# A two-block network on one core: the first mixer's head norms, its attention one step later, and its weights split ahead

## The chip, the core and the metric

The program runs on one core of one Trainium2 chip. The metric is the device time of one execution in microseconds. TensorE (PE) multiplies, VectorE (DVE) and ScalarE (ACT) work element by element, SyncE (SP) issues every DMA. Each engine runs its own list of instructions in order and waits on semaphores for the others.

## The reference, cut to what matters

Two blocks over 512 tokens of width 1024, all float32: a gated feed-forward layer (f1), a first mixer (m1), a second feed-forward layer (f2), then four more stages. The change touches f1 and m1. With the constants put in, m1 is:

```python
h = rmsnorm(x, norm_mix)
xr, gr, q, k, v, ga, gb = split(h @ w_in)            # seven parts of 1024 columns
xc = dwconv(xr)                                      # 4 taps
y_lru = (lru_scan(xc) + lru_scan_backward(xc)) * gelu(gr)   # gates of 64x64 blocks, sqrt, scan
q = rmsnorm(q per head of 64) * q_norm * 64**-0.5    # 16 heads
k = rmsnorm(k per head of 64) * k_norm
y_att = softmax(q k^T + bias over a window of 8 x 16) v
x = x + (sigmoid(ga) * y_lru + sigmoid(gb) * y_att) @ w_out
```

## The kernel before

Activations lie with the features on the 128 partitions and the 512 tokens along the free axis, so one row of weights `w_in[i]` (128 x 1024, eight blocks of 128 x 128) gives 128 features of one part. To keep float32 accuracy, both operands are split into a high part `hi` in float32r and a rest `lo`; `mm3` (L172 to L177) makes three products per block: hi by hi, lo by hi, hi by lo. A projection (`proj`) is thus 24 products of 512 columns. `wload` (L115) loads 512 KB of weights into `raw`, ACT rounds them to `whi` (L137), DVE subtracts to get `wlo` (L144). `raw`, `whi` and `wlo` have three buffers each.

`presplit` (L149) does the split ahead of time and in DRAM: per block a load into `raw`, two casts on ACT (L160), two subtractions on DVE (L161), and a DMA of the low part to DRAM (L162). From then on `wload` loads `wlo` from there (L142) and DVE has nothing to do. In the kernel before, this is done for two weights of a late stage, 28 blocks, within f2's loop of 22 steps over the hidden width; `raw`'s three buffers are shared between it and the loop's own weights.

m1 works in eight units `unit(m)`, one per pair of heads and 128 channels. A unit projects q, k, xr, v; norms q and k per head; runs the convolution, the four gate products (`lru_gates`, three products each on `xs`) and the scan; then projects gr and ga of unit m-1, gb of unit m-2; and at last scales q and k and stacks them (`stack_q`, `stack_k`). The norm (L760 to L829): the squares of 128 tokens are the stationary operand and a 128 x 2 matrix of ones per head the moving one, so that sums stand as 128 tokens by 16 columns in a bank of the pool `t` (L768); a reciprocal root; a transpose to 16 rows (L804); and eight products of 128 columns with a selecting matrix (L824) spread each root over its 64 partitions.

The attention of unit m, `attention` (L487), is a generator of ten steps. A step makes the logits of one head and 128 queries (kh, kl; L502, L503), their softmax (`softmax`, L577, two buffers of `l`), and the transposes of the step before (L516) with their split into ph and pl (L519, L520); two of the steps make the products with the values (L532). `weave` (L566) takes turns between the pieces of `unit(m)` and the steps of `attend(m - 1)`, so the attention of one unit lies under the projections of the next.

PSUM has eight banks: `m` two (projections, gates), `o` two, `t` four (logits, transposes, spread roots). A scheduler puts each engine's instructions in order from this program order and its own costs; the order is then fixed.

Of the kernel before, what the change touches and what calls it, by code (L numbers as in the profile page):

```python
# [16 lines left out]
P = 128  # L17
S = 512
# [18 lines left out]
class Split:  # L37


    def __init__(self, raw, lo):  # L40
        self.raw, self.lo, self.shape = raw, lo, raw.shape

    def __getitem__(self, i):
        return Split(self.raw[i], self.lo[i])
# [5 lines left out]
class Net:  # L50
# [98 lines left out]
    def presplit(self, name):  # L149
# [3 lines left out]
        self.ins[name] = Split(src, lo)  # L153
        for m in range(src.shape[0]):
# [332 lines left out]
    def attention(self, ap, Q, K, V, blocks, step, logits, out, mask=None, lag=1, bank=None):  # L487
# [7 lines left out]
        for t in range(len(todo) + lag + 1):  # L495
# [25 lines left out]
            if t in (4 + lag, 8 + lag):  # L521
                a = int(t > 4 + lag)
# [54 lines left out]
    def softmax(self, ap, bias):  # L577
        nc = self.nc

        def f(a, b, ps, n):  # L580
            l = ap.tile([P, n], F32, name="l", tag="l", bufs=2)
# [127 lines left out]
    def sigm2(self, ps):  # L709

        s = self.tmp("sg")
        self.nc.scalar.activation(s, ps, AF.Tanh, scale=0.5)
        return s

    def mixer1(self, nxt):
        nc, tc, ins = self.nc, self.tc, self.ins
        w_in = ins["w_in"]
        with ExitStack() as ctx:
# [18 lines left out]
            heads = c1.tile([P, 2], F32, name="heads")  # L737
            nc.sync.dma_start(heads, ins["heads"])
            t = self.wp.tile([P, 1024], F32, name="raw", tag="raw", bufs=3)
            nc.sync.dma_start(t[0:48], ins["sel"])  # L740
            sel = c1.tile([48, 1024], F32R, name="sel")
            nc.scalar.copy(sel, t[0:48])

            sp = c1.tile([48, P], F32R, name="ssp")
            nc.vector.memset(t[0:48, 0:P], 0.0)
            nc.scalar.copy(sp, t[0:48, 0:P])
# [5 lines left out]
            NR = 16  # L752
            roots = c1.tile([P, 2 * S + NR], F32, name="roots")
            ths = [roots[:, d * S : (d + 1) * S] for d in range(2)]
            ss = roots[:, 2 * S :]
            rng = [(0, 2), (0, 3), (1, 4), (2, 4)]
            off = [384, 0, 0, 640]
            HS, YA, QK, VV = {}, {}, {}, {}

            def unit(m):  # L760

                if m < KD:
                    raws, sqs = [], []

                    def sums(w):
                        for b in range(4):
                            o = 8 * w + 2 * b
                            nc.tensor.matmul(  # L768
                                st[:, o : o + 2], sqs[w][:, b * P : (b + 1) * P], heads, start=o == 0, stop=True,
                                skip_group_check=True)  # L770

                    for w in range(2):
# [37 lines left out]
                if 0 <= m - 1 < KD:  # L810
                    self.gelu_times(HS[m - 1], self.proj(w_in[KD + m - 1], h, key="gr"))
                    yield
                    s = self.sigm2(self.proj(w_in[4 * KD + m - 1], h, key="ga"))
# [517 lines left out]
```

## Time and profile before

| | us |
|---|---|
| median of three runs (lowest, highest) | 2467.26 (2466.57, 2468.57) |
| the profiled execution, its own time | 2469.19 |
| its span in the trace | 2467.4 |
| PE busy, of the span | 2403.5 (97%) |
| DVE busy | 1468.1 (60%) |
| ACT busy | 1129.9 (46%) |
| share of PE in the chain that ended last | 84% |

Products on PE are pipelined: a product of 512 columns has a length of 0.39 us in the records but the next begins 0.23 us after it. A busy share near 100% therefore doesn't say that nothing can be won; the starts of the products do. f1 lies from 0 to some 390 us, m1 from there to some 840 us, f2 from 860 to 1230 us. In m1 a unit takes 55.4 us from the third on.

### The profile page before, as it was taken

The numbers are of one execution on the slowest core, as the hardware profiler recorded it, in microseconds if no ns is written. First come the engines' busy times: TensorE is split into PE (matmuls) and PEld (weight loads), VectorE is DVE, ScalarE is ACT, GpSimd is POOL, SyncE is SP. The second block draws the span as 40 slices with busy tenths as digits, with TensorE's granted clock in tenths as the row PEclk, the third lists the DMA queues.
The fourth block names the chain that finished last, engine by engine and source line by source line (L and its number), as shares of the span: only waits on it lengthen the run. The fifth ranks groups of instructions, "written<-read, shape, count | busy, mean of one in ns | idle before, by whom it ended". The sixth has DMA issues, their size and how long they took to land.

```text
span 2467.4 us, 32211 instructions
## 1 busy us (share of the span) xinstructions
PE 2403.5 (97%) x12710; PEld 2048.5 (83%) x12710; DVE 1468.1 (60%) x2524; ACT 1129.9 (46%) x1849; POOL 39.1 (2%) x75
## 2 busy tenths in 40 slices
PE   9999999999999999999999999999999979999998
PEld 8888898777777798888988798888898859888887
DVE  5444347888888755553556665554357996555524
ACT  5223236766666544442355554333246566433322
POOL 0000000000000000000000000000001120000000
PEclk9999999999999999999999999999999999999999
DMA  4232333322222256663432222322344413223233
GB/s 151 94 102 92 94 112 119 95 88 88 80 99 84 86 204 213 214 227 95 117 118 82 85 94 69 102 95 90 101 151 150 145 53 136 69 97 101 90 96 94
DMA packets 83559, 276.08 MB, mean 112 GB/s; under 512 B 9328, under 2 KB 14064, under 8 KB 83408
## 3 DMA queue, kind: packets, MB, share of 16 engines
q1 hardware_dynamic: 83408, 274.03, 34.4%
q8 instruction: 99, 1.62, 0.3%
q14 instruction: 52, 0.43, 0.1%
HBM read 257.20 MB, written 16.80 MB: 111 GB/s over the span
## 4 chain that ended last, share of the span: by engine, by line
PE 84%; DVE 9%; ACT 4%; issue 2%; DMA 1%; POOL 0%; SPq 0%; ACTq 0%; DVEq 0%; POOLq 0%
PE psm L177 15%; PE psm L175 15%; PE psm L176 15%; PE pso L176 10%; PE pso L175 10%; PE pso L177 10%; DVE wlo L144 1%; DVE pso L1063 1%; ACT whi L137 1%; PE pst L516 1%; PE pso L532 1%; PE pst L175 1%; PE pst L176 1%; PE pst L283 1%; PE pst L177 1%
## 5 line engine op out<-in xcount | busy, mean ns | idle before, releaser
L137 ACT CAST whi<-raw 128x1024 fp32r<-128x1024 f32 (+3 forms) x402 | 408.5, 1017 | 770.3 <-issue 340.3
L144 DVE TENSOR_TENSOR wlo<-raw,whi 128x1024 fp32r<-128x1024 f32 (+2 forms) x380 | 447.7, 1179 | 311.0 <-ACT whi L137 309.9
L175 PE MATMUL psm<-hh,whi 128*128 128x512 f32 (+1 forms) x1512 | 573.2, 380 | 4.2 <-ACT hh L326 3.0
L177 PE MATMUL psm<-hl,whi 128*128 128x512 f32 (+1 forms) x1512 | 569.0, 377 | 0.1
L176 PE MATMUL psm<-hh,wlo 128*128 128x512 f32 (+1 forms) x1512 | 569.0, 376 | 0.0
L175 PEld LDWEIGHTS psm<-hh,whi 128*128 128x128 f32 x1512 | 285.7, 189 | 54.1 <-ACT hh L326 3.9
L177 PEld LDWEIGHTS psm<-hl,whi 128*128 128x128 f32 x1512 | 285.7, 189 | 49.7 <-DVE hl L327 0.7
L176 PEld LDWEIGHTS psm<-hh,wlo 128*128 128x128 f32 x1512 | 286.2, 189 | 46.5
L175 PE MATMUL pso<-hh,whi 128*128 128x512 f32 (+1 forms) x728 | 272.8, 375 | 0.9 <-ACT whi L137 0.9
L176 PE MATMUL pso<-hh,wlo 128*128 128x512 f32 (+1 forms) x728 | 272.4, 374 | 0.2 <-DVE wlo L144 0.2
L177 PE MATMUL pso<-hl,whi 128*128 128x512 f32 (+1 forms) x728 | 272.5, 374 | 0.0
L176 PE MATMUL psm<-mh,wlo 128*128 128x512 f32 (+1 forms) x506 | 172.5, 341 | 1.6 <-DVE wlo L144 1.6
L175 PE MATMUL psm<-mh,whi 128*128 128x512 f32 (+1 forms) x506 | 172.1, 340 | 0.0
L177 PE MATMUL psm<-ml,whi 128*128 128x512 f32 (+1 forms) x506 | 172.0, 340 | 0.0
L458 DVE TENSOR_TENSOR md<-pso,gp 128x512 f32<-128x512 f32 x84 | 58.0, 692 | 169.7 <-PE pso L177 168.2
L175 PEld LDWEIGHTS pso<-hh,whi 128*128 128x128 f32 x728 | 137.9, 189 | 25.1 <-ACT whi L137 1.1
L176 PEld LDWEIGHTS pso<-hh,wlo 128*128 128x128 f32 x728 | 137.9, 189 | 24.3 <-DVE wlo L144 0.4
L177 PEld LDWEIGHTS pso<-hl,whi 128*128 128x128 f32 x728 | 137.8, 189 | 24.5 <-issue 0.5
L176 PE MATMUL pso<-mh,wlo 128*128 128x256 f32 (+1 forms) x440 | 145.7, 331 | 1.3 <-DVE wlo L144 1.3
L175 PE MATMUL pso<-mh,whi 128*128 128x256 f32 (+1 forms) x440 | 145.9, 332 | 0.3 <-ACT whi L137 0.3
L177 PE MATMUL pso<-ml,whi 128*128 128x256 f32 (+1 forms) x440 | 145.8, 331 | 0.0
L176 PEld LDWEIGHTS psm<-mh,wlo 128*128 128x128 f32 x506 | 96.8, 191 | 12.6 <-DVE wlo L144 2.2
(293 smaller groups left out, 3763.5 us busy)
## 6 DMA issues: line engine op xcount, KB each, us to landing
raw<-w_up SPq DMA_DIRECT2D x88, 512.0 KB, 3.3
raw<-w_ffn_gu SPq DMA_DIRECT2D x87, 512.0 KB, 3.4
raw<-w_in SPq DMA_DIRECT2D x56, 512.0 KB, 3.3
raw<-w_ffn_down SPq DMA_DIRECT2D x40, 512.0 KB, 3.5
raw<-w_in_odd SPq DMA_DIRECT2D x40, 512.0 KB, 3.9
raw<-w_down SPq DMA_DIRECT2D x38, 512.0 KB, 3.5
raw<-w_in_even SPq DMA_DIRECT2D x24, 512.0 KB, 3.6
w_in_odd_lo<-raw SPq DMA_DIRECT2D x20, 512.0 KB, 3.0
```

What stands on the lines that cost most here:

```text
L137: nc.scalar.copy(hi, raw[:, c])
L144: nc.vector.tensor_tensor(out=lo, in0=raw[:, c], in1=hi.bitcast(F32), op=ALU.subtract)
L175: nc.tensor.matmul(out, w[0], x[0], start=start, stop=False)
L176: nc.tensor.matmul(out, w[1], x[0], start=False, stop=False)
L177: nc.tensor.matmul(out, w[0], x[1], start=False, stop=stop)
L283: self.nc.tensor.matmul(st[:, b : b + 1], sq[:, i * P : (i + 1) * P], self.ones[:, 0:1], start=new and i == 0, stop=True, skip_group_check ...
L458: nc.vector.tensor_tensor(out=md, in0=pu, in1=gp, op=ALU.mult)
L516: nc.tensor.transpose(pt[:, i * P : (i + 1) * P], p[:, i * P : (i + 1) * P], self.ident)
L532: nc.tensor.matmul(o[:, q0:q1], V[:, g, a].rearrange("p i d -> p (i d)"), p[:, c], start=first, stop=g == 3 and p is pl, skip_group_check= ...
L1063: nc.vector.scalar_tensor_tensor(t, pad[:, i : i + S], w(i), t, ALU.mult, ALU.add)
```

## The change

- **Weights.** In f1's loop `presplit` runs over 40 of the 56 blocks of `w_in` (q, k, xr, v and ga of each unit). gr and gb stay as they were: `Split` learns which blocks have a low part in DRAM.
- **Norms.** The squares are split into hi and lo and become the moving operand: per half of 256 tokens two products with a 128 x 8 matrix, and all sums of a unit add up in one bank of `o` (bank 1) as 8 rows by 256 tokens. No transpose is needed; the roots are taken on 8 x 256 and spread with four products of 256 columns. The sums are scaled on ACT, not on DVE.
- **Attention.** It starts one step later, its transposes come two steps behind the logits (three buffers of `l`), its products with the values one step later still, 13 steps in all; these use bank 0 of `o` only.
- **First unit.** The first ga projection goes to an `m` bank behind the gates and its tanh is kept, where before it held an `o` bank until the next unit.

```diff
-    def presplit(self, name):
+    def presplit(self, name, ms=None):
...
-        self.ins[name] = Split(src, lo)
-        for m in range(src.shape[0]):
+        self.ins[name] = Split(src, lo, ms)
+        for m in ms or range(src.shape[0]):
...
-    def attention(self, ap, Q, K, V, blocks, step, logits, out, mask=None, lag=1, bank=None):
+    def attention(self, ap, Q, K, V, blocks, step, logits, out, mask=None, lag=1, bank=None, late=0):
...
-            if t in (4 + lag, 8 + lag):
-                a = int(t > 4 + lag)
+            if t in (4 + lag + late, 8 + lag + late):
+                a = int(t > 4 + lag + late)
...
                     def sums(w):
-                        for b in range(4):
-                            o = 8 * w + 2 * b
-                            nc.tensor.matmul(
-                                st[:, o : o + 2], sqs[w][:, b * P : (b + 1) * P], heads, start=o == 0, stop=True,
-                                skip_group_check=True)
+                        for b, c in enumerate(HALVES):
+                            o = NR * (2 * w + b)
+                            for i, t in enumerate(sqs[w]):
+                                nc.tensor.matmul(
+                                    st[0:NR, 0:SH], heads[:, o : o + NR], t[:, c], start=w + b + i == 0,
+                                    stop=w + b + i == 3)
...
-                        sqs.append(sq)
+                        sqs.append(self.split(self.tp, sq, "R", "sq", 2))
...
-                            st = self.psum("t")
+                            st = self.psum("o", 1)
...
-                    nc.vector.tensor_scalar(ss, st[:, 0:NR], 1.0 / DH, EPS, ALU.mult, ALU.add)
+                    nc.scalar.activation(ss, st[0:NR, 0:SH], AF.Identity, bias=self.epst[0:NR], scale=1.0 / DH)
...
-                        self.ready["ga"] = self.proj(w_in[4 * KD], h, "o")
+                        SG[0] = self.sigm2(self.proj(w_in[4 * KD], h), yp)
                     nc.scalar.activation(roots, roots, AF.Sqrt)
-                    rs = c1.tile([P, NR], F32, name="rs", tag="rs", bufs=2)
-                    nc.vector.reciprocal(rs, ss)
-                    rt = self.psum("t")
-                    nc.tensor.transpose(rt[0:NR, 0:P], rs, self.ident)
-                    nc.scalar.copy(sp[0:NR], rt[0:NR, 0:P])
-                    nc.vector.tensor_tensor(
-                        out=sp[32 : 32 + NR], in0=rt[0:NR, 0:P], in1=sp[0:NR].bitcast(F32), op=ALU.subtract)
+                    nc.vector.reciprocal(ss, ss)
+                    nc.scalar.copy(sp[0:NR], ss)
+                    nc.vector.tensor_tensor(out=sp[32 : 32 + NR], in0=ss, in1=sp[0:NR].bitcast(F32), op=ALU.subtract)
...
-                        for b in range(4):
-                            o = 4 * w + b
-                            nc.tensor.matmul(
-                                bc[:, b * P : (b + 1) * P], sel[:, o * P : (o + 1) * P], sp, start=b == 0, stop=True,
-                                skip_group_check=True)
+                        for b, c in enumerate(HALVES):
+                            o = (2 * w + b) * P
+                            nc.tensor.matmul(
+                                bc[:, c], sel[:, o : o + P], sp, start=b == 0, stop=True, skip_group_check=True)
...
             def attend(m):
+                yield
...
-                return self.attention(ap, *QK.pop(m), VV.pop(m), rng, 2, self.softmax(ap, bias), put)
+                yield from self.attention(ap, *QK.pop(m), VV.pop(m), rng, 2, self.softmax(ap, bias, 3), put, None, 2, 0, 1)
...
-                self.weave((unit(m), n), (attend(m - 1) if m > 0 else None, 10))
+                self.weave((unit(m), n), (attend(m - 1) if m > 0 else None, 13))
...
             if s == "f1":
-                n.ffn(ins["w_ffn1_gu"], ins["w_ffn1_down"], nxt)
+
+                ms = [j * KD + m for m in range(KD) for j in (2, 3, 0, 6, 4)]
+                n.ffn(ins["w_ffn1_gu"], ins["w_ffn1_down"], nxt, extra=(n.presplit("w_in", ms), 40))
```

How the order of instructions moves is seen at three places. In the changed kernel, lines have numbers some two to five higher; L125 there is L123 before.

SP in f1's loop, before: after the constants come 38 loads of the loop's weights in one run, then those of the second product (`raw` is the buffer, `w_ffn_gu` and `w_ffn_down` the weights).

```order
L356 DMA x<-x 128x4x256
L92 DMA vecs<-vecs 128x494
L93 DMA ident<-ident 128x128
L123 DMA raw<-w_ffn_gu 128x1024 x38
L123 DMA raw<-w_ffn_down 128x1024 x2
```

SP at the same place, now: two steps of the loop. L158 loads a block of `w_in`, L164 stores its low part.

```order
L158 DMA raw<-w_in 128x1024 x2
L125 DMA raw<-w_ffn_gu 128x1024
L164 DMA w_in_lo<-raw 128x1024 x2
L125 DMA raw<-w_ffn_gu 128x1024
L158 DMA raw<-w_in 128x1024 x2
L125 DMA raw<-w_ffn_gu 128x1024
L164 DMA w_in_lo<-raw 128x1024 x2
L125 DMA raw<-w_ffn_gu 128x1024
```

Per step of the loop two loads and two stores are new, and the loop's own two loads stand between them: one behind the two new loads, one behind the two stores.

PE at the gates of unit 4, before: the last gates (xsh, xsl are the split convolution), the transposes of v, and at once the next projection (hh, hl are the split h).

```order
L175 MATMUL psm<-xsh,whi 128x512
L176 MATMUL psm<-xsh,wlo 128x512
L177 MATMUL psm<-xsl,whi 128x512
L545 MATMUL pst<-ident,v 128x128 x4
L175 MATMUL psm<-xsh,whi 128x512
L176 MATMUL psm<-xsh,wlo 128x512
L177 MATMUL psm<-xsl,whi 128x512
L175 MATMUL psm<-xsh,whi 128x512
L176 MATMUL psm<-xsh,wlo 128x512
L177 MATMUL psm<-xsl,whi 128x512
L175 MATMUL psm<-hh,whi 128x512
```

PE at the same place, now, from the transposes of v to the fourth gate (kh, kl with qs are logits, ident with l transposes, ph and pl with v the products with the values).

```order
L547 MATMUL pst<-ident,v 128x128 x4
L504 MATMUL pst<-kh,qs 128x256
L505 MATMUL pst<-kl,qs 128x256
L534 MATMUL pso<-ph,v 128x256
L177 MATMUL psm<-xsh,whi 128x512
L178 MATMUL psm<-xsh,wlo 128x512
L179 MATMUL psm<-xsl,whi 128x512
L518 MATMUL pst<-ident,l 128x128 x3
L534 MATMUL pso<-pl,v 128x256
L177 MATMUL psm<-xsh,whi 128x512
L178 MATMUL psm<-xsh,wlo 128x512
L179 MATMUL psm<-xsl,whi 128x512
```

Six more products with the values and three transposes follow before the next projection: between the second and third gate, the third and fourth, and the fourth and the projection there is now work of the attention.

On DVE, the end of a unit now reads: norm of q, sum of the merge, norm of k, second sum, two stacks of q, two of k, their two copies, first logits. The split of a projection's weights that stood among the stacks is gone, and the attention's last sum (L847) stands earlier.

PE at the first unit's gates, before: a quarter of the first ga projection (pso from hh, hl) stands between the sums, the transposes and the gates.

```order
L768 MATMUL pst<-heads,sq 128x2 x8
L175 MATMUL pso<-hh,whi 128x512
L176 MATMUL pso<-hh,wlo 128x512
L177 MATMUL pso<-hl,whi 128x512
L545 MATMUL pst<-ident,v 128x128 x4
L175 MATMUL pso<-hh,whi 128x512
```

PE at the first unit's gates, now.

```order
L547 MATMUL pst<-ident,v 128x128 x4
L774 MATMUL pso<-sqh,heads 8x256
L774 MATMUL pso<-sql,heads 8x256
L774 MATMUL pso<-sqh,heads 8x256
L774 MATMUL pso<-sql,heads 8x256
L177 MATMUL psm<-xsh,whi 128x512
L178 MATMUL psm<-xsh,wlo 128x512
```

There is no projection between them any more; the ga projection comes behind the fourth gate.

## Rows read from the trace of the kernel before

**Rows 1.** Windows: a stretch of f1, then of f2; columns in the first line.
```profile
core 0: us, PE busy (x) PEld busy (x) DVE busy (x) ACT busy (x) POOL busy (x), PEclk, DMA share, GB/s
120.00:220.00 100.00, 100.00 (x443) 82.83 (x442) 41.57 (x47) 29.96 (x38) 0.00 (x0) 1.00 0.29 95
940.00:1040.00 100.00, 100.00 (x443) 82.83 (x442) 55.25 (x71) 43.04 (x62) 0.00 (x0) 1.00 0.64 220
```
**Rows 2.** Windows: one unit of m1, the same columns.
```profile
586.40:641.80 55.40, 53.59 (x262) 43.12 (x262) 44.07 (x90) 36.64 (x66) 0.00 (x0) 1.00 0.26 89
```
**Rows 3.** Chain of waits in m1: start us, length us, what.
```profile
586.83 0.79 PE pst L768 x8
...
642.23 0.79 PE pst L768 x8
```
**Rows 4.** Waits of weight loads (PEld) in that unit: us in total, times, longest.
```profile
PEld pso L532 <- DVE pl L520: 1.3, 1, 1.3
PEld psm L175 <- ACT roots L666: 0.8, 2, 0.6
PEld pst L502 <- ACT kh L616: 0.8, 1, 0.8
PEld pst L503 <- DVE kl L617: 0.7, 1, 0.7
```
**Rows 5.** Timeline of PE at that unit's end: start us, length us, what, [idle before].
```profile
627.54 0.28 PE L532 MATMUL pso<-ph,v 128*128 128x256 f32 x1
627.66 0.28 PE L532 MATMUL pso<-pl,v 128*128 128x256 f32 x1
627.87 0.88 PE L824 MATMUL pst<-ssp,sel 48*128 48x128 f32 x6
...
629.49 0.39 PE L175 MATMUL psm<-hh,whi 128*128 128x512 f32 x1
...
631.99 0.39 PE L177 MATMUL psm<-hl,whi 128*128 128x512 f32 x1
632.77 0.38 PE L502 MATMUL pst<-kh,qs 128*128 128x256 f32 x1 [0.39 <-ACT kh L616]
```
**Rows 6.** DVE groups in m1 by form: count | busy us, mean ns | idle before.
```profile
L144 DVE TENSOR_TENSOR wlo<-raw,whi 128x1024 fp32r<-128x1024 f32 x57 | 69.6, 1220 | 10.3 <-ACT whi L137 10.1
L588 DVE RECIPROCAL rd<-den 128x1 f32<-128x1 f32 x64 | 10.1, 158 | 3.7 <-ACT l L586 3.6
L802 DVE RECIPROCAL rs<-roots 128x16 f32<-128x16 f32 x8 | 2.0, 246 | 0.0
```
**Rows 7.** Timeline of PE in the first unit.
```profile
404.68 1.84 PE L768 MATMUL pst<-heads,sq 128*128 128x2 f32 x16
```
**Rows 8.** Timeline of ACT in the first unit.
```profile
404.87 0.59 ACT L794 COPY v<-pso 128x512 f32<-128x512 f32 x1 [0.48 <-PE pso L177]
408.93 1.28 ACT L666 ACT_TABLE_LOAD   x1
```
**Rows 9.** Timeline of SP in f2.
```profile
971.69 4.19 SPq L156 DMA_DIRECT2D raw<-w_in_odd  x2
978.40 0.33 SPq L162 DMA_DIRECT2D w_in_odd_lo<-raw  x1
...
986.36 0.33 SPq L156 DMA_DIRECT2D raw<-w_in_odd  x1
```
**Rows 10.** Source L156: landing of the loads that presplit issues in f2.
```profile
DMA to landing us min/median/max: 3.1/3.9/4.9
```
**Rows 11.** Source L162: landing of its stores.
```profile
DMA to landing us min/median/max: 2.6/2.9/4.5
```
**Rows 12.** Timeline of ACT in f2: a pair of casts, a cast of weights.
```profile
976.43 1.14 ACT L160 CAST hi<-raw 128x512 fp32r<-128x512 f32 x2 [1.64 <-DMA raw<-w_in_odd]
978.61 1.06 ACT L137 CAST whi<-raw 128x1024 fp32r<-128x1024 f32 x1 [1.04 <-PE psm L177]
```
**Rows 13.** Timeline of DVE in f2.
```profile
977.08 1.29 DVE L161 TENSOR_TENSOR raw<-raw,hi 128x512 fp32r<-128x512 f32 x2 [0.95 <-ACT hi L160]
984.05 0.69 DVE L458 TENSOR_TENSOR md<-pso,gp 128x512 f32<-128x512 f32 x1 [1.92 <-PE pso L177]
```

More of the change, by code (lines that the diff above doesn't have):

```diff
@@ L37, with __init__ @@
 class Split:
-    def __init__(self, raw, lo):
-        self.raw, self.lo, self.shape = raw, lo, raw.shape
+    def __init__(self, raw, lo, only=None):
+        self.raw, self.lo, self.shape, self.only = raw, lo, raw.shape, only
     def __getitem__(self, i):
+        if self.only is not None and i not in self.only:
+            return self.raw[i]
         return Split(self.raw[i], self.lo[i])
@@ L494, in attention @@
         ps = {}
-        for t in range(len(todo) + lag + 1):
+        for t in range(len(todo) + lag + late + 1):
             if t < len(todo):
@@ L575, in weave, with softmax @@
                 pass
-    def softmax(self, ap, bias):
+    def softmax(self, ap, bias, bufs=2):
         nc = self.nc
         def f(a, b, ps, n):
-            l = ap.tile([P, n], F32, name="l", tag="l", bufs=2)
+            l = ap.tile([P, n], F32, name="l", tag="l", bufs=bufs)
             m = ap.tile([P, 1], F32, name="m", tag="m", bufs=8)
@@ L707, in gelu_times, with sigm2 @@
         nc.vector.tensor_tensor(out=hs, in0=t, in1=hs, op=ALU.mult)
-    def sigm2(self, ps):
-        s = self.tmp("sg")
+    def sigm2(self, ps, pool=None):
+        s = pool.tile([P, S], F32, name="sg", tag="ya", bufs=2) if pool else self.tmp("sg")
         self.nc.scalar.activation(s, ps, AF.Tanh, scale=0.5)
@@ L736, in mixer1 @@
             nc.vector.tensor_scalar(hb, self.V[:, bo : bo + bn], 0.5, None, ALU.mult)
-            heads = c1.tile([P, 2], F32, name="heads")
-            nc.sync.dma_start(heads, ins["heads"])
+            t = self.tmp("hs")
+            nc.sync.dma_start(t[:, 0:32], ins["heads"])
+            heads = c1.tile([P, 32], F32R, name="heads")
+            nc.scalar.copy(heads, t[:, 0:32])
             t = self.wp.tile([P, 1024], F32, name="raw", tag="raw", bufs=3)
[L740 to L746, printed above, removed]
+            nc.sync.dma_start(t[0:40, 0:S], ins["sel"])
+            sel = c1.tile([40, S], F32R, name="sel")
+            nc.scalar.copy(sel, t[0:40, 0:S])
+            sp = c1.tile([40, S // 2], F32R, name="ssp")
+            nc.vector.memset(t[0:40, 0 : S // 2], 0.0)
+            nc.scalar.copy(sp, t[0:40, 0 : S // 2])
             pad = c1.tile([P, S + 3], F32, name="xp")
@@ L812, in unit @@
                     yield
-                    s = self.sigm2(self.proj(w_in[4 * KD + m - 1], h, key="ga"))
+                    s = SG.pop(m - 1) if m - 1 in SG else self.sigm2(self.proj(w_in[4 * KD + m - 1], h))
                     nc.vector.scalar_tensor_tensor(HS[m - 1], s, 1.0, HS[m - 1], ALU.add, ALU.mult)
@@ L1269, in layout @@
     a["x"] = np.ascontiguousarray(A(x)[0].T.reshape(KD, P, S))
-    heads = (np.arange(P)[:, None] // DH == np.arange(2)[None]).astype(np.float32)
+    heads = np.zeros((2, DH, 2, 2, 2, 2, 2), np.float32)
+    sel = np.zeros((2, 2, 2, 2, 2, 2, 2, DH), np.float32)
+    for w in range(2):
+        for b in range(2):
+            for i in range(2):
+                heads[i, :, w, b, b, w, i] = 1.0
+                sel[:, b, w, i, w, b, i] = 1.0
+    heads, sel = heads.reshape(P, 32), sel.reshape(2, 8, S)
     tile2 = lambda v: np.tile(A(v).reshape(-1), 2)[:, None]
@@ L1285, in layout @@
     a["vecs"] = np.ascontiguousarray(np.concatenate([v for _, v in vecs], 1))
-    sel = np.zeros((2, 2, 4, 2, 8, P), np.float32)
-    for w in range(2):
-        for b in range(4):
-            for i in range(2):
-                sel[:, w, b, i, 4 * w + b, i * DH : (i + 1) * DH] = 1.0
-    sel = sel.reshape(2, 16, 1024)
-    a["heads"], a["sel"] = heads, np.concatenate([sel[0], np.zeros_like(sel[0]), sel[1]])
+    a["heads"], a["sel"] = heads, np.concatenate([sel[0], np.zeros((24, S), np.float32), sel[1]])
     a["ident"] = np.eye(P, dtype=np.float32)
```

9 lines of the change are left out of this document (5 added, 4 removed).

## The prediction, made before the changed kernel was run

> **What bounds the kernel now.** I read first the windows, then the starts of products in PE's timeline, then the chain and the waits inside m1. In f1 and f2 PE starts 443 products in every 100 us [rows 1]. A product of 512 columns takes 2.50 us / 11 = 0.227 us from start to start [rows 5], so 443 of them fill the window: f1's loop has no gap, and only more or less work on PE, or a late weight, moves it. DVE and ACT stand far below.
>
> m1 is different. From unit to unit it takes 55.4 us [rows 3]. PE's work in a unit, by starts: seven projections, 168 x 0.227 = 38.1; twelve gate products, 2.8; logits and products with the values, 16 of 256 columns at 0.12 [rows 5] and 16 of 384, by the columns 0.18, together 4.8; 24 transposes of 128 columns at 0.11, 2.6; 16 records of the norm's sums at 0.10 [rows 3], 1.6; eight spread products at (0.88 - 0.27) / 5 = 0.12 [rows 5], 1.0; one transpose, 0.1. That is 51.0 us, so 4.4 us of each unit are gaps. The waits name most of them [rows 4]: the products with the values wait for pl (1.3), the projection behind the gates for ACT to empty a bank (0.8), the first logits for kh (0.8) and kl (0.7), the latter just after the norms were spread [rows 5]. All four are data that come late for the place PE was given, on engines that are 80% (DVE, 44.07 of 55.40) and 66% busy [rows 2]. Over eight units the gaps are some 35 us, and no wait for weights is among the rows.
>
> **The change part by part.**
>
> *Norms, PE's work.* Out go 16 records at 0.10 (1.6), eight spread products at 0.12 (0.96) and a transpose (0.11). In come eight products of 256 columns for the sums and four to spread, at 0.12 each [rows 5]: 1.44. Saved are 1.23 us per unit, 9.8 in all. The bounds are 0.09 (a width of 256 streamed at 0.18 us, the next row up) and 1.5 per unit (0.10 each, the shortest row); I take 1.23, since 256 columns in float32r is the very form of the row.
>
> The row of the old sums is eight records in 0.79 us, though each has two columns only [rows 3]. The Trainium skill, "TensorE: Matmul & The Clock Gate", section "Back-to-back issue gap", gives about 60 cycles for up to 64 columns and 262 for 256. An estimate from that table is 0.4 us for the old sums and 0.87 for the new ones, so that the exchange would cost 0.5 us per unit and the time would be some 9 us above my sum. The trace doesn't bear it out for the products that go, 0.10 us and not 0.025, and these are what is removed.
>
> *Norms, other engines.* DVE gains two subtractions of 128 x 512, at 0.69 [rows 13], and loses a scale of 16 columns. The reciprocal grows from 16 to 256 columns; by the two rows it costs (246 - 158) / 15 = 5.9 ns per column, so about 1.7 us (from 0.25 to 1.7). ACT gains two casts of 512 columns at some 0.6 [rows 12], the scale of the sums and 240 columns in the root, below 2 us together. None of it is on PE's way: the sums are wanted by the spread products some 12 us after the root.
>
> *Weights.* Five of eight DVE subtractions per unit go, at 1.22 [rows 6]: 6.1 us. DVE's unit falls from 44.1 to about 44.1 - 6.1 + 1.4 + 1.4 = 40.8. In their place SP issues five loads of 512 KB per unit, which brings m1 from 89 to about 140 GB/s; f2 carries 220 [rows 1, 2]. Such a load waits on SP until PE has left that buffer, two projections (10.9 us) before the next use, and lands in some 4 us; the loads queued behind it are later ones.
>
> *Attention a step later.* kh is now wanted after the next unit's whole first projection: 4 x 0.12 + 24 x 0.227 = 5.9 us after the spread began, where it was ready 4.9 us after [rows 5]. That wait goes. kl needs on DVE two norms, two sums of the merge, four stacks and a copy, about 8 x 0.69 + 0.42 = 5.9, begun 0.5 us after the spread: it comes 0.3 to 0.6 us late. The wait for pl goes, as its transposes are two steps old when the values are wanted, and what is queued behind pl on DVE no longer matters. Behind the gates now lie six products with the values and three transposes, 6 x 0.14 + 0.33 = 1.2 us, so ACT has emptied the bank; I keep 0.3. Of 4.4 us I keep 1.7 (kl 0.6, gates 0.3, pl 0.1, the rest of the small waits 0.7) and save 2.7 in units 2 to 7: 16.2. The bounds are 0 and 4.4 per unit. Unit 1, with a larger wait at the first logits but less to lie beside it, is put at 2.0. The last attention, with 13 steps where ten were beside three projections, is put at 0 (bounds 1 either way).
>
> *First unit.* Here it loses. The first ga projection stood between sums, transposes and gates, 18 of its 24 products by the old order, 4.1 us. Now nothing stands there: PE has v's transposes at 405.5, waits for the sums' split and the convolution, and after two gates for ACT, which first loads a table for 1.28 us [rows 8]. The old sums ended where they now begin [rows 7]. The cover gone is worth 0 to 4.1; as ACT had emptied the first bank only at some 411, I take 3.4.
>
> *f1.* 40 presplits in 22 steps of 10.9 us, two in 18 of them, one in four. f2 carries 28, with 55% DVE and 0.64 of DMA, at the same 443 products [rows 1]. The loop to watch is that of the three `raw` buffers on SP: load, casts and subtractions, store, and the next load when the second store has landed. With the medians 3.9 [rows 10], 1.95 from the first cast to the end of the pair on DVE [rows 12, 13], three more DVE operations of 0.69 up to the second store, 2.9 [rows 11] and 0.3 for issue: 11.2 us against 10.9. A step with two presplits thus slips 0.3 us, 5.4 in 18; a step with one takes 3.9 + 1.95 + 2.9 = 8.8 and gives 2.1 back; and a weight that is cast when its buffer falls free is ready 10.9 - 1.06 - 1.22 = 8.6 us ahead [rows 6, 12]. So I put it at 0. The near bound is the shortest landings, 3.1 and 2.6, which leave room; the far one the longest, 4.9 and 4.5: 13.8 us, 18 x 2.9 - 8.6 - 4 x 2.1 = 35 us. f1 can't gain, since PE has no gap there.
>
> **Sum.** -9.8 - 16.2 - 2.0 + 3.4 + 0 = -24.6 us against the profiled execution's 2469.2: 2444.6. The runs' median lies 1.9 us below that execution, so the forecast is 2443.
>
> **Rivals.**
>
> *The gaps form again elsewhere.* DVE would still be at 40.8 of some 51.6 us, 79%, in the same order behind the same chains, and a wait for pl may become one for l or for the sums' split. For it: the busy shares; against it: each of the four waits has 1 to 5 us of new work before it. Then only PE's work counts, less the first unit: 2467.3 - 9.8 + 3.4 = 2461.
>
> *f1 becomes bound by its loads: slower.* One mechanism: the second store must land before the next load may take its buffer, behind it on SP stands a weight of f1's own loop, and PE waits for that. For it: in f2 two presplits in a row took 14.7 us from load to load [rows 9]. Against it: there the loop's own weights held their buffers because PE was behind. At the far bound f1 costs 35 us: 2443 + 35 = 2478. It outweighs the gain from a loop of 10.9 + (24.6 + 17) / 18 = 13.2 us on.
>
> The landings in f2 grew little at 220 GB/s [rows 10, 11]. The Trainium skill, "DMA: Bandwidth & Descriptors", section "Latency and other measured facts", gives 0.2 us of latency on average and 2 us at high load. By it a loaded read and a loaded write would each add 1.8 us; an estimate from that page is a loop of 14.8 us, 53 us in f1 and a time of 2496. The trace has nearly three times f1's present rate without that step, so this has 2 of the chances that follow.
>
> *Nearly all gaps close.* If DVE's lighter load also frees the small waits, 0.5 us per unit stays: 8 x 3.9 + 9.8 - 3.4 = 38 us, 2430. That the change doesn't do what it says is not open: the orders show fewer products and the moved steps.
>
> **Chances.** Forecast 62 in 100, with its own range 2435 to 2454 (unit 1.9 to 3.3 us saved, first unit 0 to 4.1). Gaps form again 13. Nearly all close 8. f1 slower than before 9. A loss in f1 of some 20 us, or losses in both, that leave it level 8. A measurement of this kernel can't tell 0.2%, 4.9 us, from no change. Faster by more takes the forecast, the third and most of the second: 0.81; within 0.09; slower 0.10. The range 2433 to 2462 leaves out the slow cases and the deeper half of the fast one.
>
> **What will show it.** Right: 443 products per 100 us in f1; units of 51 to 52 us from the third on; no wait of L532 for pl or of L502 for kh; a gap of 3 us at the first unit's gates; eight records of 256 columns for the sums in about 1 us. Wrong: units above 53.5 us, or a wait of f1's projections for whi, wlo or `raw`.

## The result and the profile after

| | before | changed |
|---|---|---|
| median us (runs; lowest, highest) | 2467.91 (4; 2466.57, 2468.93) | 2443.32 (4; 2441.57, 2443.98) |
| ratio, 95% interval | | 0.990 [0.988, 0.992] |
| profiled execution's span | 2467.4 | 2441.7 |

The forecast was 2443. Windows of the changed kernel, a stretch of f1 and one unit of m1 (columns as in [rows 1, 2]):

```profile
120.00:220.00 100.00, 100.00 (x443) 82.81 (x442) 59.27 (x79) 47.02 (x68) 0.00 (x0) 1.00 0.76 268
616.55:668.74 52.19, 51.19 (x250) 41.93 (x249) 40.78 (x87) 37.77 (x70) 0.00 (x0) 1.00 0.45 144
```

f1 still starts 443 products in 100 us, now at 268 GB/s in place of 95. A unit takes 52.19 us in place of 55.40, just above the 51 to 52 of the forecast, with DVE at 40.78 us in it, as worked out. PE's waits in that unit answer to [rows 4]:

```profile
PEld pso L534 <- DVE pl L522: 1.2, 1, 1.2
PEld pst L505 <- DVE kl L619: 0.6, 1, 0.6
PEld pst L826 <- issue: 0.4, 1, 0.4
```

kh (0.8 before) and the gates' bank (0.8 before) are gone, kl is nearly as it was, and pl, which the prediction had going, still costs 1.2 us. The sums of one of the two, q or k (the old eight records are in [rows 3]), are four records 0.12 us apart, two such groups in a unit:

```profile
628.93 0.28 PE L774 MATMUL pso<-sqh,heads 128*8 128x256 f32 x1
629.05 0.28 PE L774 MATMUL pso<-sql,heads 128*8 128x256 f32 x1
629.16 0.28 PE L774 MATMUL pso<-sqh,heads 128*8 128x256 f32 x1
629.28 0.28 PE L774 MATMUL pso<-sql,heads 128*8 128x256 f32 x1
```

To see where the time went I split the stretch from f1's first product with `w_ffn_down` to the first product with `w_out` into work and gaps: each record gets the spacing of its width (0.228 us for 512 columns, 0.176 for 384, 0.119 for 256, 0.110 for 128, 0.099 for fewer), and what the starts lie further apart is gap. Units are counted from one spreading of the roots to the next. The last column is the prediction's term.

| us | before | changed | difference | predicted |
|---|---|---|---|---|
| work of PE | 533.6 | 524.4 | -9.2 | -9.8 |
| gaps up to the first spreading | 1.7 | 5.9 | +4.2 | +3.4 |
| gaps, unit 1 | 6.0 | 1.8 | -4.2 | -2.0 |
| gaps, units 2 to 7 | 26.2 | 14.2 | -12.0 | -16.2 |
| gaps, last attention | 3.0 | 1.5 | -1.5 | 0 |
| start of f1's first product with `w_ffn_down` | 255.7 | 255.7 | 0.0 | 0 |

That is 22.7 us less by the end of m1; the other 3.0 of the 25.7 between the two profiles lie in stages that the change doesn't touch. By these rows each term came out within some 4 us of the prediction. They do not say which edit earned it, and there the prediction was wrong.

### The profile page after: what moved, and what is told of

It is laid out like the page before. It is cut to its first block, busy times and chain, and to the rows that moved or that the text cites. A ratio compares the mean times of both kernels' runs of the same rounds, so it can differ in the third digit from the quotient of the medians.

```text
span 2441.7 us, 32367 instructions
## 1 busy us (share of the span) xinstructions
PE 2385.8 (98%) x12606; PEld 2039.4 (84%) x12606; DVE 1492.2 (61%) x2572; ACT 1186.8 (49%) x1954; POOL 39.2 (2%) x76
## 4 chain that ended last, share of the span: by engine, by line
PE 82%; DVE 10%; ACT 5%; issue 2%; DMA 1%; POOL 0%; SPq 0%; DVEq 0%; ACTq 0%; POOLq 0%
PE psm L179 15%; PE psm L178 15%; PE psm L177 15%; PE pso L177 10%; PE pso L178 10%; PE pso L179 10%; DVE pso L1065 1%; PE pso L534 1%; ACT whi L139 1%; PE pst L518 1%; DVE wlo L146 1%; PE pst L285 1%; PE pst L177 1%; PE pst L178 1%; PE pst L179 1%
## 5 line engine op out<-in xcount | busy, mean ns | idle before, releaser
L146 DVE TENSOR_TENSOR wlo<-raw,whi 128x1024 fp32r<-128x1024 f32 (+2 forms) x341 | 399.8, 1174 | 335.5 <-ACT whi L139 332.2
L177 PEld LDWEIGHTS pso<-hh,whi 128*128 128x128 f32 x720 | 135.9, 189 | 24.6 <-ACT whi L139 1.1
L163 DVE TENSOR_TENSOR raw<-raw,hi 128x512 fp32r<-128x512 f32 x136 | 87.8, 686 | 55.0 <-ACT hi L162 55.0
```

The costliest lines, as they stand in the source:

```text
L146: nc.vector.tensor_tensor(out=lo, in0=raw[:, c], in1=hi.bitcast(F32), op=ALU.subtract)
L163: nc.vector.tensor_tensor(out=low[:, c], in0=raw[:, c], in1=hi.bitcast(F32), op=ALU.subtract)
L177: nc.tensor.matmul(out, w[0], x[0], start=start, stop=False)
```

## The experiments

Theory A is the prediction's: the norms earn their work, the later attention earns the gaps, the split weights cost nothing and earn little. The rivals give the gaps to DVE's load (B), put a cost on the loads in f1 (C, F; G denies it), give the gaps to the order that the norms bring with them (D, H), or are told with their run (E, J, K, L).

All results first. f1 is the start of its first product with `w_ffn_down`. "Gaps" are those of the table above: all, in units 1 and 2, and in the mean of units 3 to 7. The kernel before, run beside each group of runs, had medians of 2467.1 to 2467.9 us, so medians of different rows can be compared to about 1 us.

| kernel (norms N, attention L, weights P) | median us | ratio to before, 95% | f1 | work | gaps | u1+u2 | u3-7 |
|---|---|---|---|---|---|---|---|
| before | 2467.7 | | 255.7 | 533.6 | 36.9 | 10.1 | 4.40 |
| p_only (P) | 2467.74 | 1.000 [0.9991, 1.0009] | 261.6 | 533.6 | 32.4 | 8.1 | 3.96 |
| l_only (L) | 2465.17 | 0.9990 [0.9981, 0.9999] | 255.9 | 533.6 | 34.4 | 12.4 | 3.52 |
| n_only (N) | 2454.99 | 0.9948 [0.9936, 0.9961] | 254.9 | 524.4 | 32.6 | 16.2 | 2.35 |
| no_n (L, P) | 2461.99 | 0.9979 [0.9970, 0.9988] | 255.2 | 533.6 | 30.1 | 6.3 | 2.73 |
| no_p (N, L) | 2452.03 | 0.9934 [0.9921, 0.9948] | 257.0 | 524.4 | 29.6 | 11.9 | 2.03 |
| no_l (N, P) | 2450.06 | 0.9932 [0.9920, 0.9945] | 255.9 | 524.4 | 26.0 | 6.9 | 2.26 |
| changed (N, L, P) | 2443.32 | 0.990 [0.9882, 0.9917] | 255.7 | 524.4 | 23.3 | 4.6 | 2.26 |
| few_p (P: 10 blocks) | 2444.60 | 0.9909 [0.9896, 0.9923] | 257.8 | 524.4 | 22.2 | 4.6 | 2.07 |
| p56 (P: 56 blocks) | 2501.60 | 1.0138 [1.0124, 1.0152] | 311.4 | 524.4 | 24.4 | 4.7 | 2.00 |
| rt_o | 2464.51 | 0.9987 [0.9978, 0.9995] | 255.6 | 533.6 | 33.3 | 10.0 | 3.78 |
| ga_o | 2448.38 | 0.9921 [0.9909, 0.9934] | 258.7 | 524.4 | 24.4 | 8.4 | 2.36 |
| ga_o_inter | 2445.19 | 0.9910 [0.9895, 0.9926] | 256.5 | 524.4 | 22.5 | 7.6 | 1.83 |
| inter20 | 2447.46 | 0.9917 [0.9904, 0.9931] | 255.7 | 524.4 | 24.6 | 4.4 | 2.61 |

The first unit's move, the fourth part of the change, is in no_n, no_p and no_l as in the changed kernel, and not in p_only, l_only and n_only. Gaps up to the first spreading are 1.7 to 2.3 us without it and 5.7 to 7.5 with it, so a single part is read from its run against the kernel before, or from the run without it against the changed kernel, and not across the two groups.

**One part alone: the attention (l_only).** The kernel before with the last part of the change's diff that concerns the attention, both `o` banks in turn.

```diff
+                yield
...
-                return self.attention(ap, *QK.pop(m), VV.pop(m), rng, 2, self.softmax(ap, bias), put)
+                yield from self.attention(ap, *QK.pop(m), VV.pop(m), rng, 2, self.softmax(ap, bias, 3), put, None, 2, None, 1)
```

> The kernel before with the attention later alone (first step empty, transposes two steps behind, products with the values one more, three buffers of l, 13 steps; both banks of o in turn); norms and weights as before. Theory A: the gaps of a unit fall from 4.4 us to some 2, so 14 to 18 us less, 2450 to 2454 us, units of 52.7 to 53.4 us, with the first unit unchanged. Rival B (without the lighter DVE the gaps form again): units above 54.4 us and 2459 us or more, DVE at 44 us in a unit and waits for kl and pl as before.

It earned 2.6 us. PE's waits in one unit of this kernel, from 627.84 to 682.32 us:

```profile
PEld psm L175 <- ACT roots L666: 1.2, 2, 0.9
PEld pso L532 <- DVE pl L520: 0.9, 2, 0.7
PEld pst L503 <- DVE kl L617: 0.7, 1, 0.7
```

The wait for kh is gone, as predicted, but the one for the gates' bank has grown from 0.8 to 1.2 us, and those for pl (1.3 before) and kl stay. Theory A falls; B's bound of 2459 us holds.

**One part alone: the norms (n_only).** All edits of the norms; the sums stay in pool `t`, the first unit's ga where it was.

```diff
-                        sqs.append(sq)
+                        sqs.append(self.split(self.tp, sq, "R", "sq", 2))
...
-                    rt = self.psum("t")
-                    nc.tensor.transpose(rt[0:NR, 0:P], rs, self.ident)
```

> The kernel before with the new norms alone (squares split, sums as 8 rows of 256 tokens in a bank of pool t, no transpose, four spread products); attention, weights and the first unit as before. Theory A (the norms' gain is PE's work): 1.23 us less in each of eight units, 2467.9 - 9.8 = 2458 us, units of 54.2 us. Rival B (DVE, which gets two subtractions and a longer reciprocal, is already late in a unit): the 2.8 us more on DVE stand in front of the gates or of pl and eat the gain, 2463 to 2470 us, with the waits for kl, pl or the bank of the gates longer than before.

It earned 12.7 us, more than the 9.2 us of work that it removes. In units 3 to 7 its gaps are 2.35 us, nearly the whole change's 2.26: so in steady units the norms alone close the gaps that the prediction gave to the attention. PE's longest waits in one such unit, from 623.63 to 675.75 us:

```profile
PEld pst L516 <- issue: 1.6, 2, 1.0
PEld pst L516 <- DVE l L589: 0.4, 1, 0.4
PEld pst L503 <- DVE kl L617: 0.3, 1, 0.3
```

Neither kh nor pl is waited for any more, with the attention at its old steps. In units 1 and 2 the new norms open 6.0 us of new gaps. Waits there, from 428 to 520 us, then DVE's timeline (start, length) with the weight that PE waits for at the end, and PE's first product with it:

```profile
PEld psm L176 <- DVE wlo L144: 5.0, 2, 2.7
PEld psm L175 <- ACT qr L779: 2.5, 1, 2.5
```

```profile
474.12 0.68 DVE L615 TENSOR_TENSOR kl<-qr,kh 64x512 fp32r<-64x512 f32 x1
474.72 0.68 DVE L170 TENSOR_TENSOR sql<-sq,sqh 128x512 fp32r<-128x512 f32 x1
...
477.52 1.23 DVE L144 TENSOR_TENSOR wlo<-raw,whi 128x1024 fp32r<-128x1024 f32 x1
```

```profile
478.80 0.79 PE L176 MATMUL psm<-hh,wlo 128*128 128x512 f32 x1 [1.96 <-DVE wlo L144]
```

wlo is made behind the stacks, the new subtraction sql and a softmax step, without a pause, and PE stands still for it. Theory A's 2458 us is missed by 3 us on the fast side, and rival B was right in this place only.

**One part alone: the weights (p_only).**

```diff
+                ms = [j * KD + m for m in range(KD) for j in (2, 3, 0, 6, 4)]
+                n.ffn(ins["w_ffn1_gu"], ins["w_ffn1_down"], nxt, extra=(n.presplit("w_in", ms), 40))
```

> The kernel before with 40 of the 56 blocks of w_in split ahead in f1 alone. Theory A: f1 keeps 443 products per 100 us, so it costs nothing there; in m1 kl comes earlier by the subtraction of 1.22 us that stood among the stacks, which ends the wait of 0.7 for it, and the rest stays: 2460 to 2466 us, units of 54.4 to 55.2 us. Rival B (DVE's load is what makes the gaps): 2457 us or less, the waits of pl and kh shorter too. Rival C (f1 bound by its loads): 2470 us or more with a wait of f1's projections for whi, wlo or raw.

The time did not move, above Theory A's 2460 to 2466 us, yet the profile holds two movements: m1 has 4.5 us fewer gaps, and f1 ended 5.9 us later. PE's waits in f1 from 60 to 256 us; the changed kernel has none in that stretch:

```profile
PEld psm L178 <- DVE wlo L146: 4.6, 6, 1.1
PEld psm L177 <- ACT whi L139: 0.8, 1, 0.8
```

In both programs the instructions of f1 stand in the same order on PE, ACT, DVE and SP, so what differs is how long transfers took: the loads of `w_in` landed in 5.5 us here (median, 60 to 250 us) and in 5.2 in the changed kernel. Rival C is half right: its waits came, its time of 2470 us did not. f1 is at its edge.

**The change without one part (no_p, no_l, no_n).** The three diffs are those above, the other way round.

```diff
-                ms = [j * KD + m for m in range(KD) for j in (2, 3, 0, 6, 4)]
-                n.ffn(ins["w_ffn1_gu"], ins["w_ffn1_down"], nxt, extra=(n.presplit("w_in", ms), 40))
+                n.ffn(ins["w_ffn1_gu"], ins["w_ffn1_down"], nxt)
```

> The changed kernel without the weights split ahead: f1 as before the change, and in m1 DVE makes wlo of all eight weights of a unit again. Theory A (the parts add up: the gaps went because the attention was put later, DVE's load matters little): 2443 to 2448 us, units of 52.1 to 52.7 us with DVE at some 46.9 us in them (40.8 and five subtractions of 1.22). Rival B (it is the lighter DVE that lets pl, kl and the roots come in time): each unit loses at least the 1.2 us of a subtraction that stands before kl or the sums, so 2453 us or more, units above 53.3 us, and longer waits for kl and pl. Rival C (splitting ahead costs something in f1 that m1 pays for): below 2441 us.

```diff
-                yield
...
-                yield from self.attention(ap, *QK.pop(m), VV.pop(m), rng, 2, self.softmax(ap, bias, 3), put, None, 2, 0, 1)
+                return self.attention(ap, *QK.pop(m), VV.pop(m), rng, 2, self.softmax(ap, bias, 2), put, None, 1, 0, 0)
```

> The changed kernel with the attention back at its old steps (no empty step first, transposes one step behind, products with the values one step later as before, two buffers of l, ten steps), norms and weights as changed. Theory A of the prediction (the gaps go because the attention is later): 14 to 18 us above the changed kernel, 2457 to 2461 us, units of 54.2 us with waits for kh and pl. Theory D, formed from the first four runs (the norms alone already gave units of 52.1 us, and the split weights remove the waits for wlo in units 1 and 2): 2443 to 2448 us, units of 51.8 to 52.4 us. Rival E (the later step still pays for the small waits): 2449 to 2455 us.

```diff
-                        sqs.append(self.split(self.tp, sq, "R", "sq", 2))
+                        sqs.append(sq)
...
+                    rt = self.psum("t")
+                    nc.tensor.transpose(rt[0:NR, 0:P], rs, self.ident)
```

> The changed kernel with the old norms (sums of 128 tokens in 16 columns, in a bank of pool t, transpose of the roots, eight spread products), attention and weights as changed. Theory A of the prediction: 9.8 us of PE's work come back, 2453 us, units of 53.4 us. Theory D (with the old norms the order puts the first logits early, as the run with the attention alone had units of 54.5 us): units of 54 us or more and 2458 to 2465 us.

Without P: 8.7 us lost, 6.3 of them gaps, with units 3 to 7 even a little better (2.03); the loss is in units 1 and 2, where gaps go from 4.6 to 11.9. Waits of no_p from 428 to 520 us:

```profile
PEld psm L176 <- DVE wlo L144: 3.4, 2, 1.7
PEld pst L502 <- ACT kh L616: 2.9, 2, 1.7
```

Theory A (2443 to 2448) is out, and so is B's picture of a loss in every unit. Without L: 6.7 us lost by the medians, 2.7 by the gaps, 2.3 of them in units 1 and 2. Its profiled execution was the fastest of its five (2445.93, the slowest 2453.12); where the others lost the rest no trace shows; f1 could be the place, but that isn't shown. In steady units nothing is lost (2.26 both): the values' place in the order doesn't matter there once the norms are new. One unit's waits of no_l (618.91 to 670.99 us):

```profile
PEld pst L518 <- issue: 1.8, 3, 1.0
PEld pst L505 <- DVE kl L619: 0.4, 1, 0.4
...
PEld pso L534 <- DVE pl L522: 0.2, 1, 0.2
```

The wait for pl is 0.2 us here and 1.2 in the changed kernel: the later attention, which was to end it, brings it back, and closes in exchange the one of 1.8 us in front of the transposes.

Without N: 18.7 us lost, 9.2 of work, 6.8 of gaps, the rest between profiles. Theory D is right in its range of time for no_n, with a unit of 53.8 us just under its 54, and 2 us low for no_l. There the median lies in rival E's 2449 to 2455; the small waits that E names for it don't show in the steady units.

**Fewer and more blocks (few_p, p56).**

```diff
-                ms = [j * KD + m for m in range(KD) for j in (2, 3, 0, 6, 4)]
+                ms = [j * KD + m for m in (1, 2) for j in (2, 3, 0, 6, 4)]
...
```

> The changed kernel with ten blocks split ahead in f1 in place of 40: the five weights of units 1 and 2 only; DVE makes wlo of the others in m1. Theory D (the split weights earn only where PE waited for wlo, in units 1 and 2; later units run at 51.9 us without them): 2440 to 2446 us. Rival B (the lighter DVE earns in every unit): 2448 us or more, units above 52.5 us. Theory F (f1 with 40 blocks stands at its edge and costs up to 6 us in some runs): with ten the step of f1 is 10.88 us throughout, and the runs lie closer together than those of the changed kernel.

```diff
-                ms = [j * KD + m for m in range(KD) for j in (2, 3, 0, 6, 4)]
+                ms = [j * KD + m for m in range(KD) for j in (2, 3, 0, 6, 4, 1, 5)]
...
```

> The changed kernel with all 56 blocks of w_in split ahead in f1, in 22 steps: two or three in a step. The loop of the raw buffers (load, casts, subtractions, store, next load) is asked for 2.5 turns in a step of 10.88 us. Theory F (with 40 blocks the loop is at its edge: steps of 12.4 us for two blocks were seen where a step had time to give): some 56 x 6.2 = 347 us of loop against 22 x 10.88 = 239, so that f1 ends 60 to 110 us later, 2500 to 2550 us, with waits of f1's products for whi and wlo. Rival G (the loop has room left, since steps of one block gave back what others lost): f1 at most 10 us later, 2440 to 2453 us.

Ten blocks earn in m1 what 40 do (22.2 us of gaps against 23.3), with DVE at 46.07 us in a unit again. B falls; D holds. f1's loop kept its step of 10.88 us throughout; that its end stands at 257.8 comes from its start, since the steady steps begin at 51.1 us, before at 48.9. That the runs lie closer together, as F had it, can't be said: 1.9 us apart here, 2.4 in the changed kernel. The window of few_p's unit:

```profile
sum 51.85, PE 51.22 PEld 41.83 DVE 46.07 ACT 37.87 POOL 0.00; mean PE 51.22 PEld 41.83 DVE 46.07 ACT 37.87 POOL 0.00
```

With 56 blocks f1 ends 56 us later. PE's waits in p56 from 60 to 310 us, and its window:

```profile
PEld psm L177 <- ACT whi L139: 25.8, 10, 4.2
PEld psm L178 <- DVE wlo L146: 10.8, 10, 1.2
```

```profile
60.00:300.00 240.00, 210.97 (x866) 168.05 (x865) 136.73 (x181) 110.55 (x164) 0.00 (x0) 0.96 0.80 279
```

361 products per 100 us in place of 443, at 279 GB/s against 268 with 40 blocks. This is the second rival of the prediction, f1 bound by its loads, shown at 2.5 blocks in a step; at 1.8 it has only begun. Theory F holds, near its lower end, and G is out.

**A freed bank (rt_o).** The kernel before with one word changed.

```diff
-                    rt = self.psum("t")
+                    rt = self.psum("o")
```

> The kernel before with one word changed: the transpose of the norm's roots writes to a bank of the pool o instead of the pool t. Nothing else; no work less on PE. In the order the logits and transposes that stood behind that transpose, 36 products after the last gate, now stand directly behind the gates, as in the kernel with the new norms alone. Theory H (a good part of what the new norms gained came from this freed bank, not from fewer products): the gap of 0.47 us behind the gates goes and the wait for pl becomes shorter, 0.5 to 1.2 us in seven units, 2459 to 2464 us. Rival A (the norms gain by PE's work alone): no change, 2466 to 2469 us.

It earned 3.3 us with no work removed. PE behind the last gate, before and then in rt_o (start, length, what, [idle before]):

```profile
661.54 0.39 PE L177 MATMUL psm<-xsl,whi 128*128 128x512 f32 x1
662.13 0.50 PE L175 MATMUL psm<-hh,whi 128*128 128x512 f32 x1 [0.20 <-ACT roots L666]
```

```profile
659.72 0.40 PE L177 MATMUL psm<-xsl,whi 128*128 128x512 f32 x1
659.95 0.33 PE L502 MATMUL pst<-kh,qs 128*128 128x384 f32 x1
...
660.87 0.39 PE L175 MATMUL psm<-hh,whi 128*128 128x512 f32 x1
```

The bank of `t` that the transposed roots held kept four logits and three transposes behind them, 36 products later. Freed, they stand behind the gates, cover ACT's emptying of the bank, and the gap of 0.47 is gone. Theory H holds. The new norms have no such transpose, so they get this for nothing. It is 0.62 of the 2.05 us that they close in a steady unit. For another part the order shows the cause, but no run isolates it: with the new norms the first logits stand 26 products behind the spreading, where they stood 15 behind it before, and the wait for kh goes. The other runs agree: PE waits 0.8 to 1.0 us for kh in a steady unit where 13 or 15 products lie between (p_only, before, rt_o), 0.2 with 19 (no_l), and not at all with 24 or more. What closes the rest is open.

**The first unit's cover (ga_o) and the stacks (ga_o_inter).**

```diff
-                            st = self.psum("o", 1)
+                            st = self.psum("t")
...
-                        SG[0] = self.sigm2(self.proj(w_in[4 * KD], h), yp)
+                        self.ready["ga"] = self.proj(w_in[4 * KD], h, "o")
...
```

> The changed kernel with the first unit's ga projection back in a bank of the pool o, where it lies between the sums and the gates; for that the sums go to the pool t and the attention takes both o banks in turn. Theory A (the first unit's cover is worth 3.4 us): of the 3.6 us of waits for the squares' low part and the gates' bank 0.2 to 0.5 stay, 2439 to 2441 us. Rival J (the sums in t push the logits later, and the bank that ga holds does the same to unit 1): the gain is lost in units 1 and 2, 2442 to 2446 us.

The waits of the first unit do go (5.9 to 2.7 us of gaps, of which 1.6 lie at f1's end in both), but unit 1 has 5.7 in place of 1.8, and the run is 5 us slower than the changed kernel, with f1 3.0 later in the profile. The gain is lost as rival J says, though the time lies 2.4 us above its range. So the first unit's move, with its banks, loses 3.2 us in the first unit and wins 3.9 in the next. PE's waits in unit 1:

```profile
449.72 0.50 PE L177 MATMUL psm<-xsh,whi 128*128 128x512 f32 x1 [0.30 <-ACT roots L668]
452.36 0.55 PE L518 MATMUL pst<-ident,l 128*128 128x128 f32 x3 [0.62 <-DVE l L591]
454.08 0.44 PE L518 MATMUL pst<-ident,l 128*128 128x128 f32 x2 [0.74 <-DVE l L591]
```

ga_o_inter is ga_o with the stacks of q and k made head by head:

```diff
-                    QK[m] = self.stack_q(ap, raws[0], 2), self.stack_k(ap, raws[1], 4, nc.vector.tensor_copy)
+                    QK[m] = self.stack_qk(ap, raws[0], raws[1])
```

`stack_qk` makes q, kh and kl of the first head, then those of the second.

> As the run before it, and besides q and k are stacked head by head (qs, kl of the first head, then of the second), so that the first kl is ready one operation of 0.7 us sooner. Theory K (PE's wait for kl, 0.4 to 0.5 us in each of seven units, is that one operation): 3 us below the run before it, 2436 to 2438 us, units of 51.6 us. Rival L (the wait passes on to the second head's qs or to pl): the same as the run before it within 1 us.

The steady gaps are 0.53 us smaller per unit and the wait for kl is gone from them: there theory K holds, not L. The median is 3.2 us below ga_o's, as K has it, but of the 4.6 us between the two profiles 2.2 are f1's, and units 1 and 2 keep most of what ga_o lost; K's 2436 to 2438 us is missed.

**A version for both (inter20).** The changed kernel with the stacks by head and 20 blocks, so that f1 has one in a step.

```diff
-                ms = [j * KD + m for m in range(KD) for j in (2, 3, 0, 6, 4)]
+                ms = [j * KD + m for m in range(1, 5) for j in (2, 3, 0, 6, 4)]
...
```

> The changed kernel (first unit, banks and attention as changed) with two edits: 20 blocks split ahead in f1, those of units 1 to 4, one in a step but for the first; and q and k stacked head by head. From the runs so far: f1 keeps its step of 10.88 us and loses nothing in its loop (40 blocks cost 0.4 to 6 us there), the wait for kl of 0.5 us goes in the units whose weights are split ahead (units of 51.7 us in place of 52.1, in the others 51.9), so some 2 to 3 us less than the changed kernel: 2440 to 2442 us. Rival: the units with DVE making wlo again lose as much at kl as the others gain, 2443 to 2445 us.

f1's step is 10.88 throughout and units 3 and 4 take 51.65 us, as expected. But units 5 and 6, the first whose weights DVE splits again, take 53.6, and the time lies above both ranges that were expected. PE's waits from 616 to 690 us:

```profile
PEld psm L178 <- DVE wlo L146: 3.8, 2, 1.9
PEld pso L534 <- DVE pl L522: 1.2, 1, 1.2
```

In no_p the same wait came in units 1 and 2, in few_p (first such unit 3) not at all, and why it skips few_p is open. No version was faster than the changed kernel.

## Why the prediction came out, and where it was wrong

- *Norms, PE's work:* -9.2 for -9.8. The new records are 0.12 us apart, the old 0.10 [rows 3], so that the sums alone went from 1.6 to 1.0 us, and work fell by 1.15 us in each of eight units. The prediction's estimate from the table of the Trainium skill ("TensorE: Matmul & The Clock Gate", "Back-to-back issue gap"), which holds for a single isolated product, made the exchange of the sums a loss of 0.5 us per unit. The trace disagrees.
- *Norms, other engines:* "None of it is on PE's way" failed. With the new norms alone, 6.0 us of new gaps open in units 1 and 2, most of them for a wlo that DVE makes behind the squares' subtraction and the stacks; with the weights split ahead they are gone. No run takes that subtraction out alone. The reciprocal came out at 1.73 us (1.7 worked out) and lies, with the scans, in front of the last pl of a unit, where the wait of 1.2 us remains. DVE in the changed kernel, and PE after it:

```profile
658.25 1.73 DVE L807 RECIPROCAL roots<-roots 8x256 f32<-8x256 f32 x1
...
661.60 1.22 DVE L693 TENSOR_TENSOR_SCAN wx<-nq,wx 128x512 f32<-128x512 f32 x1
662.73 1.20 DVE L694 TENSOR_TENSOR_SCAN wx<-nq,wx 128x512 f32<-128x512 f32 x1
...
665.37 0.42 DVE L522 TENSOR_TENSOR pl<-pst,ph 128x256 fp32r<-128x256 f32 x1
```

```profile
665.84 0.44 PE L534 MATMUL pso<-pl,v 128*128 128x384 f32 x1 [0.76 <-DVE pl L522]
```

- *Attention later, -18.2:* this step failed. The gaps of units 1 to 7 did shrink by 16.2 us, but the attention earned 2 of them. Each part's share of these gaps, once against the kernel before and once against the changed kernel:

| gaps closed in units 1 to 7, us | part alone | part left out |
|---|---|---|
| attention | 2.1 | 2.3 |
| norms | 4.2 | 4.0 |
| weights | 4.3 | 6.2 |
| first unit's move, with its banks (ga_o) | - | 4.3 |

The right column adds up to 16.8, near the 16.2 of all parts together; each figure rests on one profiled execution. I had taken "wanted later in the program" for "wanted later on PE": the order of the engine is set by banks and by the scheduler, and a bank that was freed elsewhere moved the logits as far as the new steps did. "What is queued behind pl no longer matters" was wrong with it: with the later attention PE waits 0.9 to 1.4 us for pl in a steady unit, with the new norms and the old attention 0.2 or nothing.
- *kh and kl:* their sizes were right; kl was put at 0.3 to 0.6 late and waits 0.6. But the wait for kh goes with the norms alone as well.
- *Weights:* "DVE 40.8" was right, but the sum has no term for what they earn in m1: 4.5 us of all gaps alone, 6.3 beside the other parts, and there in units 1 and 2.
- *First unit, +3.4:* 4.2 of gaps. The waits are the ones named, for the squares' split and, after the table load, for the gates' bank; what the move wins back in unit 1 was not seen:

```profile
408.23 0.29 PE L774 MATMUL pso<-sql,heads 128*8 128x256 f32 x1 [1.08 <-DVE sql L172]
411.36 0.50 PE L177 MATMUL psm<-xsh,whi 128*128 128x512 f32 x1 [1.20 <-ACT roots L668]
```

- *f1, 0:* 0.0 in this profile, but with less margin than I had. The loads of `w_in` land in 5.2 us, not in the 3.9 taken from [rows 10]; the stores in 3.1 (2.9 in [rows 11]). From 60 to 250 us of the changed kernel (count, KB, median us to landing), and SP's load of two pairs:

```profile
w_in_lo<-raw SPq DMA_DIRECT2D x31, 512.0 KB, 3.1
raw<-w_in SPq DMA_DIRECT2D x31, 512.0 KB, 5.2
```

```profile
89.08 1.65 SPq L158 DMA_DIRECT2D raw<-w_in  x2
...
100.81 0.81 SPq L158 DMA_DIRECT2D raw<-w_in  x2
```

With 5.2 and 3.1 in the sum the loop is 12.6 us (its terms gave 11.1, not 11.2), and these pairs follow 11.7 us apart, against a step of 10.88. By an estimate from that, 18 steps with two blocks slip 14 us, just inside the 17 us of slack that the prediction counted in its weights and the four single steps. The loads rose by 1.3 us and the stores by 0.2 at 268 GB/s; the 220 of f2 that the prediction leant on were 2.3 times f1's rate, not nearly three. The Trainium skill ("DMA: Bandwidth & Descriptors", "Latency and other measured facts") has the latency of memory rise to 2 us at high load; by the prediction's estimate from it f1 would have ended 53 us later, which this run doesn't show.
- *Rivals:* "the gaps form again" is true of pl alone; "nearly all close" is not, since 2.3 us of gaps stay in a steady unit, where that rival had 0.5.

So the total was right by luck, with errors that offset each other: the attention's term was some 16 us too large, and what the norms, the weights and the first unit's move close in the same units, 4, 4 to 6 and 4 us, was put at next to nothing.

## What to carry to other kernels

The gaps here hung on PE's order, and the order in part on who holds a bank: before crediting a gain to the edit that was meant for it, run each part alone and each left out, and count work and gaps apart. An edit that loads a helper engine (the new norms on DVE) can have its price in a few units only, where another edit pays for it; ten split blocks in the right two units were worth as much as 40. A loop at 1.8 turns per step with 76% of the DMA engines' time looked free in one profile and cost 5 us in another.

## What was not expected of the hardware

f1 with the same 40 blocks in the same order reached its first product with `w_ffn_down` at 255.2, 255.7, 255.9, 256.5, 258.7 and 261.6 us in six profiles. In the first three every steady step takes 10.88 us; in the others steps grow by up to 1.2 us, 0.8, 2.8 and 5.3 in all. Without the blocks no step grows in five profiles, and f1's end lies between 254.9 and 257.0 by its start alone. The profiles are from several chips, and whether the chip or the execution makes the difference isn't shown. The stages behind m1, which no kernel here changes, took 1629.4 to 1632.9 us up to PE's last product from profile to profile, so that 3 us of the difference between the two profiles can't be given to the change.
